# Sixty-four bytes of padding between two SBUF pools of a one-core encoder kernel

## The chip, the cores and the metric

The kernel runs on one core of one Trainium2 chip. The metric is device time in microseconds (us); lower is better. A time is the median of several runs; the rows below come from one profiled execution of the same program.

## What is computed

Two encoder blocks over 256 tokens of 1,024 channels, all in float32. `rms` is a root-mean-square norm with a learned gain. Each mixer has three attention groups (latent attention with 8 heads, windowed attention with 4, neighbourhood attention with 4).

```python
for l in range(2):
    x = x + 0.5 * swiglu(rms(x, ffn1_norm[l]), ffn1_w_in[l], ffn1_w_out[l])      # 1024 -> 2 x 2816 -> 1024
    z = rms(x, mix_norm[l]) @ w_mix_in[l]
    o = concat(rms(latent(z)), rms(windowed(z)), rms(neighbourhood(z)))
    x = x + o @ w_mix_out[l]
    x = x + attention_to_memory(rms(x, mem_norm_x[l]), rms(mem, mem_norm_m[l]))
    x = x + 0.5 * swiglu(rms(x, ffn2_norm[l]), ffn2_w_in[l], ffn2_w_out[l])
    x = rms(x, block_norm[l])
```

## The kernel before

**The weight stream.** All weights come from HBM in pieces of [128 partitions x up to 1,024 floats], in the order of use. `emit_split` (L125) loads a piece into a tile `raw` (pool `rawp`), ScalarE rounds it to float32r as `whi` (L136), and VectorE makes the remainder `wlo` (L137); both lie in the pool `wp`, 7 tiles each. A piece is loaded three ahead of its use. The activations are split in the same way into a high and a low tile, so a product of float32 precision is three float32r matmuls: high by high, high by low, low by high.

**The two ways in which a matmul gets its operands.** TensorE loads one operand as stationary weights (LDWEIGHTS, 128 columns) and streams the other past it. In `mm3` calls of the feed-forward and of the projections (L163 to L165, and L318 for the first columns) the 128x128 block of `whi` or `wlo` is stationary and an activation tile of 256 columns is streamed. In `formb` (L524 to L526), in the two latent up-projections (L699 to L701, L753 to L755) and in the products of the memory tokens it is the other way round: a 128-column block of an activation tile is stationary and 256, 384, 416 or 512 columns of a weight tile are streamed. By the shapes in the code both layers together have 2,384 blocks of the first kind (or memory products) with three matmuls each, 384 matmuls in `formb` and 72 in the up-projections: 7,608 matmuls that pair a weight tile with an activation tile. 7,248 of them stream 256 columns.

**Where tiles lie.** The pools are laid out one after another in each partition: `cp` (residual, gains, constants), `rawp`, `wp`, `sp` (ten slots of 8,192 bytes for the activations), `tp` (working tiles of 128 to 2,048 bytes), `mp` (small ones). A slot of `rawp` or `wp` has 4,096 bytes. The sizes of `rawp`, `wp` and `sp` are multiples of 512 bytes, so every `raw`, `whi`, `wlo` and every activation tile of `sp` starts at the same address modulo 512. A stationary block of 128 floats is 512 bytes and a streamed tile of 256 floats is 1,024, so the operands of nearly every one of these matmuls start at one address modulo 512. The exception is the piece `mb0` in `formb`: it holds two K tiles of 416 columns (1,664 bytes), so the stream of an odd K tile starts 128 bytes further modulo 512 than that of an even one.

**Order.** The framework orders the instructions of each engine by a simulated timeline (`schedule_with_timeline_sim=True`). GpSimd (POOL) starts with small memsets (`nhalf`, L107; a column of ones in `memV`, L541), and waits for the first data after them.

Of the kernel before, what the change touches and what calls it, by code (L numbers as in the profile page):

```python
# [17 lines left out]
L = 2  # L18
# [10 lines left out]
# where in the attention's pipeline (after which head) other work is put in  # L29
# [5 lines left out]
# columns of the per-partition parameter block, per layer  # L35
G_F1, G_MIX, G_MX, G_MM, G_F2, G_BLK, G_GRP, G_CQ, G_HEAD = 0, 8, 16, 24, 32, 40, 48, 56, 59
NG = 67
# columns of the per-token (replicated) parameter block, per layer
# [4 lines left out]
def weight_plan():  # L43
    """Names and widths of the pieces of the weight stream, in the order of use."""
    plan = []
    for l in range(L):
        for name, count, width in (
            ("f1i", 2 * NJ, 1024), ("f1o", NJ, 1024), ("mc", 3, 1024), ("mb0", 4, 832), ("uq", 2, 768),
            ("mb1", 4, 1024), ("ukv", 1, 1024), ("mb2", 4, 768), ("kvk", 2, 1024), ("mo", 8, 1024),
            ("wq", 2, 1024), ("kvv", 2, 1024), ("wo", 2, 1024), ("f2i", 2 * NJ, 1024), ("f2o", NJ, 1024),  # L50
        ):
            plan += [(name, l, i, width) for i in range(count)]
    return plan


def mo_order():
    """(column tile, K tile) of the mixers' output projection: the later groups' K tiles come first."""
    o = [(i, k) for i in range(6) for k in range(4, 8)]
    o += [(i, k) for i in range(6) for k in range(4)]
    return o + [(i, k) for i in range(6, 8) for k in (4, 5, 6, 7, 0, 1, 2, 3)]  # L60
# [8 lines left out]
def encoder_kernel(ctx: ExitStack, tc: tile.TileContext, gxT, memT, wst, bparams, consts, nab, out):  # L69
# [4 lines left out]
    wp = ctx.enter_context(tc.tile_pool(name="wp", bufs=7))  # L74
    sp = ctx.enter_context(tc.tile_pool(name="sp", bufs=10))
    tp = ctx.enter_context(tc.tile_pool(name="tp", bufs=2))
    mp = ctx.enter_context(tc.tile_pool(name="mp", bufs=9))
    pacc = ctx.enter_context(tc.tile_pool(name="pacc", bufs=8, space=PSUM))

# [30 lines left out]
    # the tensor engine's clock is gated until it has been busy for a while: busy it until the first data are there  # L110
# [43 lines left out]
    def units(kind, count):  # L154
        """Successive [128 x 128] blocks of the stream as (hi, lo)."""
        for u in range(count):
            if u % 8 == 0:
                hi, lo = piece(kind)
            o = (u % 8) * P
            yield hi[:, o : o + P], lo[:, o : o + P]  # L160
# [17 lines left out]
    class Normed:  # L178
        """hi / lo parts of (x * gain), tile by tile, and the rows' reciprocal norms.

        With pre, x stands for its own normed value with the gains pre: the rows then have two factors.
        """
# [13 lines left out]
        def _sum(self, v, keep):  # L196
            """Adds up squares, all but the last keep of them."""
            while len(v) > keep + 1:
                if len(v[0]) == 1:
                    t = tp.tile([P, T], F32, tag="sqs", bufs=3, name=self.name + "s")  # L200
                    v[0:2] = [(t, self.eng.tensor_tensor(t, v[0][0], v[1][0], ALU.add))]
                else:
                    t = v[0][0]
                    v[0:2] = [(t, self.eng.tensor_tensor(t, t, v[1][0], ALU.add))]
# [34 lines left out]
        def stats(self, r=None):  # L239
            """Means over the channels (and eps), and the factors from them: [tokens of a half, half]."""  # L240
            self.total()
            ps = acc(self.name + "ps")
            for n, v in enumerate(self.sums):
                for t in range(2):
                    s = slice(t * P, (t + 1) * P)
                    for m, q in enumerate(v):
                        nc.tensor.matmul(
                            ps[:, 2 * n + t : 2 * n + t + 1], q[0][:, s], cmean[:, 0:1],
                            start=m == 0, stop=m == len(v) - 1,
                        )  # L250
            self.m = mp.tile([P, 2], F32, tag="r", name=self.name + "m")
            nc.vector.tensor_scalar(self.m, ps[:, 0:2], EPS, None, ALU.add)
            if self.factor:
                self.r = mp.tile([P, 2], F32, tag="r", name=self.name + "r") if r is None else r
            if self.pre is None:
                if self.factor:
                    rsqrt(self.r, self.m, 2)
                return
            # both norms at once: (m2 / m + eps) ** -0.5 * m ** -0.5 = (m2 + eps * m) ** -0.5
            m2 = small(2, self.name + "m2")  # L260
            nc.vector.scalar_tensor_tensor(m2, self.m, EPS, ps[:, 2:4], ALU.mult, ALU.add)
            self.r0 = mp.tile([P, 2], F32, tag="r", name=self.name + "r0")
            rsqrt(self.r, m2, 2)
            rsqrt(self.r0, self.m, 2)

        def bcast(self):
            """The factors along the tokens, on every partition."""
            rs = [self.r] if self.pre is None else [self.r, self.r0]
            ps = acc(self.name + "pb")
            out = []  # L270
            for n, r in enumerate(rs):
                for t in range(2):
                    o = n * T + t * P
                    nc.tensor.transpose(ps[:, o : o + P], r[:, t : t + 1].to_broadcast([P, P]), ident)
                rb = tp.tile([P, T], F32, tag="rb", name=f"{self.name}rb{n}")
                nc.scalar.copy(rb, ps[:, n * T : (n + 1) * T])
                out.append(rb)
            return out
# [4 lines left out]
    def bc(ap, n):  # L283
        """[P, a, ...] -> [P, a, ..., n] by repetition."""
        return ap.unsqueeze(len(ap.shape)).to_broadcast(list(ap.shape) + [n])

# [1 line left out]
    def ffn(l, which, nx, nxt, hook=None):  # L288
# [18 lines left out]
        for j in range(NJ):  # L307
            if j == 0:
                # the tiles of x may still be in the making: two columns at once, K tile by K tile
# [49 lines left out]
    def project(nm, kind, order, nk, ah, al, nn, hooks={}, late=False):  # L359
        """x += W a in the given order of (column tile, K tile)."""  # L360
# [30 lines left out]
    class Pair:  # L391
        """Two heads whose outputs share a bank; o[:, t, cols[c], :] gets them."""
# [84 lines left out]
    def attend(heads, hooks={}, d1=AT["d1"], d2=AT["d2"]):  # L477
        """Heads in a software pipeline."""
# [16 lines left out]
    def head_factors(nm, hs, n, dim, e):  # L495
        """The heads' factors: of values that are r times what hs [P, 2, n] sums the squares of,
        r * (r ** 2 * hs / dim + eps) ** -0.5 = (hs / dim + e) ** -0.5 with e = eps / r ** 2."""
# [14 lines left out]
    def formb(nm, kind, width, kper, xh, xl, hooks={}):  # L512
        """[tokens, width] products of the next pieces, a bank for each half of the tokens."""
# [16 lines left out]
    def head_squares(nm, ps, a, n, dim, dst):  # L530
        """Sums of squares of n heads from column a of ps into dst."""
# [12 lines left out]
    class Memory:  # L544
        """Keys and values of the memory tokens; their rows' factors serve all layers."""
# [13 lines left out]
        def steps(self, kind, n, done):  # L559
            """The next n of the 16 products (a half of the tokens, a K tile) that make keys or values."""  # L560
# [53 lines left out]
    def mixer(l, nx, mem):  # L614
        nm = f"mx{l}"
        # low-rank projections, transposed
# [17 lines left out]
        # rotary tables with the gains; the softmax scale goes on the queries' gains  # L634
# [18 lines left out]
        # rows' factors of the two latents  # L653
# [18 lines left out]
        # the rotary keys, over the factors of the latent ones  # L672
# [13 lines left out]
        # latent up-projection of the queries  # L686
# [38 lines left out]
        # heads, transposed: two to a block in the windowed and the neighbourhood group  # L725
# [19 lines left out]
        # latent up-projection of the keys and values  # L745
# [29 lines left out]
        # values of the other two groups  # L775
# [25 lines left out]
        for pr in range(2):  # L801
            # heads pr and pr + 2 lie in one block and read the two kv heads
# [80 lines left out]
    def mem_attn(l, nx, mem, nxt):  # L883
# [15 lines left out]
        # the memory tokens' values fill the time until the queries are normed  # L899
# [69 lines left out]
    # the halves of the tokens in banks of their own: only the last tile's squares are waited for  # L969
# [22 lines left out]
def _tiles(v):  # L992
    """[n] -> [128, n / 128]"""
    return v.reshape(-1, P).T


def _pack_weights(inp):
    def units_a(w, order_cols):
        """w [K, N] as [128, 128] blocks, one column tile after another, K inside."""
        K = w.shape[0]  # L1000
        b = w.reshape(K // P, P, w.shape[1] // P, P)
        return b[:, :, order_cols, :].transpose(1, 2, 0, 3).reshape(P, -1)

    def rows(w):
        """w [K, N] -> [128, K / 128 * N]"""
# [5 lines left out]
    def units_in(w):  # L1011
        """Gates and values in turn; the blocks of the first four column tiles go by K tile."""
# [37 lines left out]
def _constants():  # L1050
    """Identity, rotary tables and the windowed group's biases: shapes alone decide them."""
# [17 lines left out]
def _na_bias(rel):  # L1069
    """rel [L, 4, 15, 31] gathered over (query, key); outside the window a constant."""  # L1070
# [56 lines left out]
```

## Time and profile before

| | |
|---|---|
| median of 3 runs | 1081.56 us (1080.64 to 1082.23) |
| profiled execution, first to last instruction | 1081.2 us |
| TensorE busy | 1062.2 us, 98% |
| VectorE, ScalarE, GpSimd busy | 66%, 51%, 11% |
| matmuls in the trace | 8,480 |
| read from HBM | 179.38 MB, 167 GB/s over the span |

The profiled execution shows no time beside its span. Matmuls are pipelined and their ends are modelled, so the times between the starts of matmuls say more than the busy share. PEclk is the granted clock of TensorE in tenths of its upper level (2.4 GHz; the lower one is 1.2 GHz).

### The profile page before, as it was taken

What the parts mean: (1) busy time and instruction counts of PE and PEld (TensorE: products, weight loads), DVE (VectorE), ACT (ScalarE), POOL (GpSimd) and SP (SyncE); (2) the same over time, 40 slices, a digit from 0 to 9 for tenths busy, and PEclk for the clock granted to TensorE, in tenths of its full rate; (3) what the DMA queues carried; (4) which work ended last, traced back from release to release, by engine and by line L of the source; (5) the groups of instructions that cost most, each with busy time, mean ns of one, the idle gap of its engine ahead of it and who ended that gap; (6) DMA issues with size and microseconds to landing.
All of it is one profiled execution on the core that took longest, in us unless ns stands there. A gap on an engine that the chain in (4) does not pass through costs nothing.

```text
span 1081.2 us, 20915 instructions
## 1 busy us (share of the span) xinstructions
PE 1062.2 (98%) x8480; PEld 1041.3 (96%) x8480; DVE 718.1 (66%) x1249; ACT 556.2 (51%) x928; POOL 114.3 (11%) x106
## 2 busy tenths in 40 slices
PE   8999999999999999999999999999999999999996
PEld 7999999998998999999999999999889999999996
DVE  7866667678776676666658665666886776666652
ACT  5644455556563554445445444546674555444441
POOL 4000000062030400000000000001500322000000
PEclk9999999999999999999999999999999999999999
DMA  8855556555032655555555555555531526655641
GB/s 274 274 183 188 176 198 195 170 177 192 21 120 76 231 178 187 184 179 188 181 176 178 191 177 185 202 177 173 175 127 41 156 74 223 189 179 183 187 119 40
DMA packets 54529, 181.79 MB, mean 168 GB/s; under 512 B 6048, under 2 KB 8992, under 8 KB 54432
## 3 DMA queue, kind: packets, MB, share of 16 engines
q1 hardware_dynamic: 54432, 180.45, 52.3%
q8 instruction: 66, 1.08, 0.4%
q14 instruction: 31, 0.25, 0.1%
HBM read 179.38 MB, written 1.05 MB: 167 GB/s over the span
## 4 chain that ended last, share of the span: by engine, by line
PE 73%; issue 17%; DVE 4%; POOL 2%; DMA 2%; ACT 1%; SPq 0%; POOLq 0%; DVEq 0%; ACTq 0%
PE f01i L163 4%; PE f11i L163 4%; PE f01i L165 4%; PE f01i L164 4%; PE f11i L164 4%; PE f11i L165 4%; PE f02i L163 3%; PE f02i L164 3%; PE f02i L165 3%; PE f11o L165 2%; PE f11o L164 2%; PE f11o L163 2%; PE f02o L165 2%; PE f02o L164 2%; PE f02o L163 2%
## 5 line engine op out<-in xcount | busy, mean ns | idle before, releaser
L137 DVE TENSOR_TENSOR wlo<-raw,whi 128x1024 fp32r<-128x1024 f32 (+4 forms) x337 | 407.0, 1211 | 230.7 <-ACT whi L136 229.4
L136 ACT CAST whi<-raw 128x1024 fp32r<-128x1024 f32 (+4 forms) x337 | 343.5, 1022 | 384.4 <-issue 103.9
L163 PE MATMUL f11i<-n10h,whi 128*128 128x256 f32 x320 | 90.8, 284 | 0.0
L163 PE MATMUL f12i<-n21h,whi 128*128 128x256 f32 x320 | 90.7, 284 | 0.0
L163 PE MATMUL f02i<-n20h,whi 128*128 128x256 f32 x320 | 90.7, 283 | 0.0
L163 PE MATMUL f01i<-n0h,whi 128*128 128x256 f32 x320 | 90.7, 283 | 0.0
L165 PE MATMUL f01i<-n0h,wlo 128*128 128x256 f32 x320 | 90.6, 283 | 0.0
L164 PE MATMUL f02i<-n20l,whi 128*128 128x256 f32 x320 | 90.6, 283 | 0.0
L164 PE MATMUL f01i<-n0l,whi 128*128 128x256 f32 x320 | 90.5, 283 | 0.0
L164 PE MATMUL f12i<-n21l,whi 128*128 128x256 f32 x320 | 90.5, 283 | 0.0
L165 PE MATMUL f12i<-n21h,wlo 128*128 128x256 f32 x320 | 90.5, 283 | 0.0
L165 PE MATMUL f02i<-n20h,wlo 128*128 128x256 f32 x320 | 90.5, 283 | 0.0
L164 PE MATMUL f11i<-n10l,whi 128*128 128x256 f32 x320 | 90.5, 283 | 0.0
L165 PE MATMUL f11i<-n10h,wlo 128*128 128x256 f32 x320 | 90.5, 283 | 0.0
L164 PEld LDWEIGHTS f12i<-n21l,whi 128*128 128x128 f32 x320 | 61.4, 192 | 0.0
L164 PEld LDWEIGHTS f02i<-n20l,whi 128*128 128x128 f32 x320 | 61.4, 192 | 0.0
L164 PEld LDWEIGHTS f01i<-n0l,whi 128*128 128x128 f32 x320 | 61.4, 192 | 0.0
L165 PEld LDWEIGHTS f02i<-n20h,wlo 128*128 128x128 f32 x320 | 61.4, 192 | 0.0
L163 PEld LDWEIGHTS f02i<-n20h,whi 128*128 128x128 f32 x320 | 61.4, 192 | 0.0
L164 PEld LDWEIGHTS f11i<-n10l,whi 128*128 128x128 f32 x320 | 61.4, 192 | 0.0
L165 PEld LDWEIGHTS f01i<-n0h,wlo 128*128 128x128 f32 x320 | 61.4, 192 | 0.0
L163 PEld LDWEIGHTS f12i<-n21h,whi 128*128 128x128 f32 x320 | 61.4, 192 | 0.0
(1025 smaller groups left out, 2977.0 us busy)
## 6 DMA issues: line engine op xcount, KB each, us to landing
raw<-in_w SPq DMA_DIRECT2D x311, 512.0 KB, 4.3
raw<-in_w SPq DMA_DIRECT2D x12, 384.0 KB, 3.5
raw<-in_w SPq DMA_DIRECT2D x8, 416.0 KB, 3.2
kv0mt<-in_mem SPq DMA_DIRECT2D x8, 128.0 KB, 4.2
kv1mt<-in_mem SPq DMA_DIRECT2D x8, 128.0 KB, 3.3
gx<-in_gx SPq DMA_DIRECT2D x3, 256.0 KB, 7.2
out<-gx SPq DMA_DIRECT2D x3, 256.0 KB, 2.8
gx<-in_gx SPq DMA_DIRECT2D x1, 323.0 KB, 3.0
```

What stands on the lines that cost most here:

```text
L136: ins = nc.scalar.copy(hi[:, a:b], r[:, a:b])
L137: nc.vector.tensor_tensor(lo[:, a:b], r[:, a:b], hi[:, a:b].bitcast(F32), ALU.subtract)
L163: nc.tensor.matmul(ps, ah, bh, start=first, stop=False)
L164: nc.tensor.matmul(ps, ah, bl, start=False, stop=False)
L165: return nc.tensor.matmul(ps, al, bh, start=False, stop=last)
```

## The change

A pool `pad` with one tile of [128 x 16] float32, 64 bytes in each partition, is put between the weights' pool `wp` and the activations' pool `sp`, and GpSimd fills it with zeros at the start. Nothing reads it. All tiles of `sp`, `tp` and `mp` then lie 64 bytes further in their partitions; `cp`, `rawp` and `wp` stay where they were. The rest of the diff blanks comments and docstrings, line for line, and changes no instruction.

```diff
     wp = ctx.enter_context(tc.tile_pool(name="wp", bufs=7))
+
+    pad = ctx.enter_context(tc.tile_pool(name="pad", bufs=1))
     sp = ctx.enter_context(tc.tile_pool(name="sp", bufs=10))
     tp = ctx.enter_context(tc.tile_pool(name="tp", bufs=2))
     mp = ctx.enter_context(tc.tile_pool(name="mp", bufs=9))
     pacc = ctx.enter_context(tc.tile_pool(name="pacc", bufs=8, space=PSUM))
 
+    nc.gpsimd.memset(pad.tile([P, 16], F32, name="pad"), 0.0)
+
     def slot(shape, dt, name):
```

## Rows read from the trace of the kernel before

**Rows 1.** Page: span, engines (busy us, share, instructions), granted clock in 40 slices.

```profile
span 1081.2 us, 20915 instructions
PE 1062.2 (98%) x8480; PEld 1041.3 (96%) x8480; DVE 718.1 (66%) x1249; ACT 556.2 (51%) x928; POOL 114.3 (11%) x106
...
PEclk9999999999999999999999999999999999999999
```

**Rows 2.** Page: shares of the chain of work that ended last, by engine.

```profile
PE 73%; issue 17%; DVE 4%; POOL 2%; DMA 2%; ACT 1%; SPq 0%; POOLq 0%; DVEq 0%; ACTq 0%
```

**Rows 3.** Stretches: length, busy us (count) of five engines, PEclk, DMA share, GB/s.

```profile
19.00:144.00 125.00, 125.00 (x1044) 125.00 (x1044) 83.54 (x117) 64.31 (x93) 3.57 (x5) 1.00 0.63 207
...
290.00:345.00 55.00, 53.51 (x439) 51.57 (x439) 37.07 (x76) 24.42 (x49) 10.83 (x10) 1.00 0.31 97
345.00:475.00 130.00, 128.90 (x1075) 128.70 (x1074) 86.15 (x129) 67.59 (x102) 12.59 (x8) 1.00 0.56 183
...
540.00:677.00 137.00, 137.00 (x1145) 137.00 (x1145) 86.19 (x128) 64.87 (x96) 2.29 (x2) 1.00 0.56 181
...
1010.00:1074.00 64.00, 61.89 (x517) 61.69 (x515) 27.73 (x40) 23.04 (x32) 0.69 (x1) 1.00 0.35 100
```

**Rows 4.** Timeline of TensorE, feed-forward: first and last of 27 matmuls, 256 columns.

```profile
399.77 0.28 PE L164 MATMUL f02i<-n20l,whi 128*128 128x256 f32 x1
...
400.01 0.28 PE L163 MATMUL f02i<-n20h,whi 128*128 128x256 f32 x1
...
402.89 0.28 PE L163 MATMUL f02i<-n20h,whi 128*128 128x256 f32 x1
```

**Rows 5.** Timeline of the weight loads in the same stretch.

```profile
400.02 0.19 PEld L164 LDWEIGHTS f02i<-n20l,whi 128*128 128x128 f32 x1
```

**Rows 6.** Timeline of TensorE: first and last of 13 matmuls, 384 columns.

```profile
221.73 0.33 PE L701 MATMUL mx0uq<-whi,mx0chl 128*128 128x384 f32 x1
...
223.81 0.33 PE L701 MATMUL mx0uq<-whi,mx0chl 128*128 128x384 f32 x1
```

**Rows 7.** Timeline of TensorE: first and last of 13 matmuls, 512 columns.

```profile
229.24 0.39 PE L526 MATMUL mx0mb<-whi,nx0l 128*128 128x512 f32 x1
...
231.96 0.39 PE L526 MATMUL mx0mb<-whi,nx0l 128*128 128x512 f32 x1
```

**Rows 8.** Timeline of TensorE: each first of six matmuls, 416 columns, K tiles 2 to 7.

```profile
212.15 0.35 PE L524 MATMUL mx0mb<-whi,nx0h 128*128 128x416 f32 x1
...
213.28 0.35 PE L524 MATMUL mx0mb<-whi,nx0h 128*128 128x416 f32 x1
...
214.41 0.35 PE L524 MATMUL mx0mb<-whi,nx0h 128*128 128x416 f32 x1
...
215.54 0.35 PE L524 MATMUL mx0mb<-whi,nx0h 128*128 128x416 f32 x1
...
216.67 0.35 PE L524 MATMUL mx0mb<-whi,nx0h 128*128 128x416 f32 x1
...
217.80 0.35 PE L524 MATMUL mx0mb<-whi,nx0h 128*128 128x416 f32 x1
...
218.93 0.28 PE L658 MATMUL mx0pm<-cmean,mx0csq 128*128 128x1 f32 x2
```

**Rows 9.** Line 214 on VectorE: count, ns min/median/max, first and last start.

```profile
L214 DVE SCALAR_TENSOR_TENSOR nx0l<-gx,nx0h x8: 476/479/484, 148.4 to 203.4; 128x256 fp32r<-128x256 f32 x8
L214 DVE SCALAR_TENSOR_TENSOR kv0l<-kv0mt,gx,kv0h x8: 477/479/486, 151.3 to 206.9; 128x256 fp32r<-128x256 f32 x8
```

**Rows 10.** Line 443: what VectorE waited for longest there (us, times).

```profile
  DMA mx1sw11bt<-in_consts: 1.7, 1
```

**Rows 11.** Timeline of POOL at the start: last memsets, first work (idle before, releaser).

```profile
0.72 0.11 POOL L107 MEMSET nhalf<- 128x16 f32 x1 [0.29 <-POOLq L1117]
0.76 0.11 POOL L541 MEMSET memV<- 128x8 f32 x1
3.84 1.28 POOL L644 TENSOR_SCALAR mx0gq<-gx 128x1 f32<-128x1 f32 x3 [2.97 <-DMA gx<-in_gx]
```

## The prediction

> **What bounds the kernel now.** I read the page first. TensorE is busy for 98% of the span at the upper clock level, 2.4 GHz, in all forty slices, and VectorE, ScalarE and POOL for 66%, 51% and 11% [rows 1]. The chain of work that ended last is TensorE's for 73% and "issue" for 17%, time in which the engine waits for nothing that the profile shows [rows 2]; in a full TensorE stream, that is the piece of each step which the modelled matmul does not explain. The table by stretches then says where this holds: in the feed-forwards TensorE has no gap at all (1,044 matmuls in 125 us, 1,145 in 137 us, 119.7 ns each). Gaps appear around the attention and at the starts and ends of norms, and are small: 1.5, 1.1 and 2.1 us in the stretches shown [rows 3].
>
> So the time is a count of matmuls times the step from one start to the next, and the timeline gives that step. With 256 columns, 26 steps take 3.12 us: 120.0 ns [rows 4]. The 7,248 matmuls of this width alone make 7,248 x 0.120 = 870 us of the 1081.2. With 384 columns, 12 steps take 2.08 us, 173.3 ns [rows 6]; with 512 columns, 2.72 us, 226.7 ns [rows 7]. The differences are 53.3 ns for each 128 columns, which at 2.4 GHz is one column a cycle. Taking that off (106.7, 160.0 and 213.3 ns) leaves the same 13.3 ns in all three: a fixed part of each matmul, 11% of a step of 120 ns. The next weights are loaded while a matmul streams (a load starts at 400.02 us, the matmul before it at 400.01) [rows 4, 5]. Nothing but a change of the 120 ns can move this kernel much.
>
> **The change, part by part.**
>
> *The shift between stationary and streamed operands.* It touches each of the 7,608 matmuls that pair a weight tile with an activation tile: before, both start at one address modulo 512; after, they are 64 bytes apart. It does not touch pairs of two activation tiles (scores, values), which move together, nor the split of the weights, whose three tiles stay. The price is 7,608 times the change of the step. Each 0.1 ns is 0.76 us, so 0.28 ns would be 0.2% of the time (2.2 us), about what a measurement of this kernel can tell from no change, since the three runs shown span 1.6 us.
>
> No row shows a matmul with a 64-byte shift. The nearest are those of 416 columns, where odd K tiles stream from 128 bytes further than even ones, against the same stationary phase. Six matmuls of an even K tile take 1.13 us and six of an odd one 1.13 us, in all six groups from 212.15 to 218.93 us: 188.3 ns each [rows 8]. Rounded to 0.01 us in six, the two kinds differ by at most 1.7 ns each. And the fixed part of 13.3 ns is one number for 256, 384 and 512 columns, though the streams end at different times against the load that runs beside them [rows 4, 6, 7]. A collision of two reads in one stretch of 512 bytes should show in one of these; a fixed cost of changing the weights would look just like this.
>
> Bounds, then: 1.7 ns on either side by that row, 7,608 x 1.7 = 12.9 us, so 1068 to 1094 us. The row is also what I take the value from: its two phases agree to the last digit shown, so 0 ns and 0 us. 416 columns also has the odd cost that 188.3 - 173.3 = 15.0 ns remain there instead of 13.3. It is the only width that is no multiple of 128 columns, and I come back to it as a rival.
>
> *The other engines' operands.* VectorE and ScalarE read and write the shifted tiles beside unshifted ones (`x`, the gains). The remainder of line 214 reads `x` from `cp` in one group and a memory tile from `tp` in another, 264 bytes apart modulo 512 by the sizes in the code: 479 ns both, 476 to 486 in all [rows 9]. I take 0. If each shifted operation cost 2% more, VectorE would still be idle for a third of the time [rows 1]; where it ends a wait, those 2% of 0.48 us are 0.01 us for each link of the chain. VectorE's 4% of it, 43 us, would give 0.9 us [rows 2].
>
> *DMAs.* The stream into `raw` keeps its addresses, as do the residual and the output. Sixteen loads of memory tiles and sixteen of biases land 64 bytes further. Before, the longest wait at line 443 for a bias was 1.7 us, once [rows 10]. I cost the change at 0, hidden by loading three heads ahead; uncovered it would be a part of such a wait, below 1 us.
>
> *The memset.* One more instruction on POOL, of `nhalf`'s shape: 0.11 us, with 0.04 us from start to start there. It stands before two memsets that nobody waits for soon, and POOL then sits for 2.97 us until the first data land at 3.84 us [rows 11]. Cost 0; without that cover 0.11 us. It queues no DMA and adds no wait to another engine, and `sp` keeps its slots.
>
> Sum: 1081.2 + 0 + 0 + 0 + 0 = 1081.2 us for a profiled execution. The median of the runs is 0.4 us above that, so 1081.6 us.
>
> **The rivals.**
>
> *The fixed part is a collision, and the shift ends it (faster).* In every pair of operands of the three clean widths, both start at one phase, and the next weights are read while the stream runs [rows 4, 5]. If the 13.3 ns were the two reads meeting in the same part of 512 bytes, 64 bytes could free them: up to 7,608 x 13.3 = 101 us, 980 us. For it: no row has another phase than 0 or 128 bytes. Against it: at 128 bytes the step did not fall [rows 8]. It decides as soon as a step falls by 0.28 ns. The Trainium skill, TensorE: Matmul & The Clock Gate, section Back-to-back issue gap, gives an isolated matmul 1/2.4 ns a column plus 2.5 ns, 109.2 ns for 256 columns. By that rule all but 2.5 ns of the fixed part is avoidable, and an estimate by it would be 1081.6 - 7,608 x 10.8 ns = 999 us; the trace's 120.0 ns does not agree with it for this stream.
>
> *A stream out of step with the loads costs more (slower).* With 416 columns, where a stream's end does not fall on a multiple of 512 bytes, the remainder is 15.0 ns instead of 13.3 [rows 4, 8]. If that is the price of a stream and a load that do not start at one phase, the shift puts it on all 7,608: 1.7 x 7,608 = 12.9 us, 1094.5 us, decided from 0.28 ns on. For it: that row; against it: there the end is out of step and not the start, and the odd K tiles, whose start is, cost the same as the even.
>
> *A small gain by the same lever.* The mirror of it, up to 12.9 us, 1068.7 us.
>
> *Another order.* The framework plans with a simulated timeline, and a memset at its start, if it shifted one wait there, could swap instructions. The price would be one exposed gap like those of 1.1 to 2.1 us [rows 3]: 1082.7 to 1083.7 us.
>
> *The change doesn't shift.* If the allocator rounds the pool up to 512 bytes, nothing moves: 1081.6 us.
>
> The Trainium skill, SBUF — State Buffer, section Who interferes with whom, gives TensorE two SBUF read ports of its own, one for the stream and one for the weights, and has it wait for nobody. By that rule the first three rivals fall away and the time stays at 1081.6 us. The equal steps of even and odd K tiles agree [rows 8], but no row here has 64 bytes.
>
> **How the numbers follow.** No change of the step, or no shift: 0.67, 1081.6 us, with 1079.4 to 1083.8 as its own range. The slower rival 0.12, the collision that ends 0.12, the small gain 0.05, another order 0.04, three quarters of it within 0.2%. That gives faster by over 0.2% 0.12 + 0.05 = 0.17, within 0.2% 0.67 + 0.03 = 0.70, slower 0.12 + 0.01 = 0.13. The range reaches to the bounds of the unknown step, 1068 to 1095 us, and leaves out the collision that ends, of 0.12.
>
> **What would show it.** The timeline of a feed-forward with 120.0 ns from start to start, six matmuls of 416 columns in 1.13 us, 479 ns at line 214, and 13.3 ns left at 384 and 512 columns would show each step right. A step of 121.7 ns or of 118.3 everywhere speaks for the two small rivals, one near 107 to 109 for the collision. Unequal steps in one feed-forward and not in another would mean that the phase matters together with something I haven't read. Equal steps with another sum would mean another order. My prediction is wrong if 64 bytes, which no row tried, are not like 128.

## The result and the profile after

The changed kernel takes 1067.39 us (median of four runs, 1066.59 to 1071.27) and the kernel before 1081.1 us beside it (1080.58 to 1082.23): a ratio of 0.988, 95% interval 0.986 to 0.990. It is 13.7 us faster. The profiled execution of the changed kernel took 1071.27 us itself, the slowest of the four, with a span of 1069.5 us. Its lines are numbered four higher than those of before, so L163 is now L167.

The page of the changed kernel: span, engines, granted clock in 40 slices, and the chain of work that ended last.

```profile
span 1069.5 us, 20916 instructions
...
PE 1048.8 (98%) x8480; PEld 1027.0 (96%) x8480; DVE 717.6 (67%) x1249; ACT 556.9 (52%) x928; POOL 114.5 (11%) x107
...
PEclk9999999999999999999999999999999999999998
...
PE 75%; issue 17%; DVE 4%; DMA 2%; ACT 1%; POOL 1%; SPq 0%; POOLq 0%; DVEq 0%; ACTq 0%
```

The same number of matmuls, VectorE and ScalarE instructions run, one POOL instruction more, and the shares hardly moved [rows 1, 2]. TensorE alone has become 13.4 us less busy. The table by stretches shows it at work without a gap in the feed-forwards, as before [rows 3], but with more matmuls in the same time: 121 us hold 1,031 (117.4 ns each), 136 us hold 1,158 (117.4), where it was 119.7. (Columns: length, busy us and count of PE, PEld, DVE, ACT, POOL, granted clock, DMA share, GB/s.)

```profile
19.00:140.00 121.00, 121.00 (x1031) 121.00 (x1030) 82.33 (x116) 63.02 (x93) 2.54 (x3) 1.00 0.67 212
...
363.40:366.80 3.40, 3.40 (x19) 3.40 (x18) 1.04 (x1) 0.00 (x0) 1.61 (x1) 0.53 0.69 225
534.00:670.00 136.00, 136.00 (x1158) 136.00 (x1157) 87.52 (x131) 66.50 (x99) 2.29 (x2) 1.00 0.57 185
889.10:892.50 3.40, 3.40 (x18) 3.40 (x18) 0.62 (x1) 1.04 (x1) 0.00 (x0) 0.53 0.87 299
```

The timeline of TensorE in the changed kernel, the first and the last of each row of equal matmuls (start, us, engine, line, operation, output and operands):

```profile
209.88 0.38 PE L528 MATMUL mx0mb<-whi,nx0h 128*128 128x416 f32 x1
...
211.04 0.35 PE L528 MATMUL mx0mb<-whi,nx0h 128*128 128x416 f32 x1
...
212.18 0.38 PE L528 MATMUL mx0mb<-whi,nx0h 128*128 128x416 f32 x1
...
213.34 0.35 PE L528 MATMUL mx0mb<-whi,nx0h 128*128 128x416 f32 x1
...
214.47 0.28 PE L662 MATMUL mx0pm<-cmean,mx0csq 128*128 128x1 f32 x2
...
215.71 0.34 PE L705 MATMUL mx0uq<-whi,mx0chl 128*128 128x384 f32 x1
...
217.79 0.34 PE L705 MATMUL mx0uq<-whi,mx0chl 128*128 128x384 f32 x1
...
219.52 0.39 PE L528 MATMUL mx0mb<-whi,nx0h 128*128 128x512 f32 x1
...
222.32 0.39 PE L528 MATMUL mx0mb<-whi,nx0h 128*128 128x512 f32 x1
...
362.21 0.61 PE L251 MATMUL n20ps<-cmean,n20s 128*128 128x1 f32 x4 [1.68 <-POOL n20s L208]
...
363.22 0.42 PE L168 MATMUL f02i<-n20l,whi 128*128 128x256 f32 x1
...
366.63 0.28 PE L169 MATMUL f02i<-n20h,wlo 128*128 128x256 f32 x1
...
394.78 0.28 PE L169 MATMUL f02i<-n20h,wlo 128*128 128x256 f32 x1
...
397.84 0.28 PE L168 MATMUL f02i<-n20l,whi 128*128 128x256 f32 x1
```

- **256 columns, activations streamed** (the 6,960 matmuls of the feed-forwards and projections): 26 steps in 3.06 us, 117.7 ns, where it was 120.0 [rows 4]. Over all 2,112 matmuls of the feed-forwards' output projections the mean is 117.78 ns.
- **384 columns, weights streamed**: in the query projection 12 steps in 2.08 us, 173.3 ns, as before [rows 6]. In the other product of this width, in `formb`, the first layer has 12 steps in 2.12 us, 176.7 ns; the second has 173.3 again. Before, both settled at 173.3.

```profile
234.18 0.34 PE L528 MATMUL mx0mb<-whi,nx0h 128*128 128x384 f32 x1
...
236.30 0.34 PE L528 MATMUL mx0mb<-whi,nx0h 128*128 128x384 f32 x1
```

- **512 columns, weights streamed**: 12 steps in 2.80 us, 233.3 ns, and so 6.6 ns slower [rows 7].
- **416 columns**: six matmuls of an even K tile (from 209.88 and 212.18 us) take 1.16 us, six of an odd one (from 211.04 and 213.34) 1.14 and 1.13. Before, both took 1.13 [rows 8].

So the padding changed the step of nearly everything that streams past weights, in both directions. The sum, with those steps: 6,960 x -2.2 ns = -15.3 us; the 96 query projections of the memory attention, 120 to 114 ns, -0.6; 192 products of the memory tokens, -0.4; 120 matmuls of 512 columns, +0.8; those of 416 columns, +0.2; the 48 of 384 columns in the first layer, 3.3 ns each, +0.2: together -15.1 us. Part of it is given back. TensorE waits a little longer for the sums of squares from POOL at the two norms ahead of a second feed-forward (1.7 us, as at 362.21, and 2.1 us; before 1.1 and 1.3), 1.4 us more. And after each of those gaps the granted clock falls to the lower of its two levels, 1.2 GHz, for 3.4 us (0.53 over the stretch): 16 steps from 363.22 to 366.63 take 3.41 us, 213 ns each, 1.53 us more than at 117.8, twice. -15.1 + 1.4 + 3.1 = -10.6 us; the profiled spans differ by 11.7. The other runs, 3.4 to 4.7 us faster than this one, met fewer such stretches, by their mean granted clock of 0.996 to 0.997 against 0.994 here (one stretch at half the clock is 0.0016 of the span). The execution of before that was profiled had none [rows 1].

The length of the gap doesn't settle whether the clock falls. In minus64, a kernel of the next section, the gap at the same place was longer, and the clock stayed at the upper level:

```profile
355.18 0.61 PE L249 MATMUL n20ps<-cmean,n20s 128*128 128x1 f32 x4 [2.01 <-POOL n20s L206]
```

```profile
355.20:358.60 3.40, 3.40 (x29) 1.00 0.88 300
```

At the lower level the fixed part of the step is gone: 213 ns are 256 cycles at 1.2 GHz, one for each column. Whether that holds at distance 0 isn't shown: in the feed-forwards of the kernel before the record has no stretch at the lower level.

What the prediction costed at nothing did stay at nothing. Line 218 on VectorE (count; ns at least, in the median, at most):

```profile
L218 DVE SCALAR_TENSOR_TENSOR nx0l<-gx,nx0h x8: 477/480/484, 145.1 to 199.3; 128x256 fp32r<-128x256 f32 x8
L218 DVE SCALAR_TENSOR_TENSOR kv0l<-kv0mt,gx,kv0h x8: 478/480/486, 147.9 to 203.1; 128x256 fp32r<-128x256 f32 x8
```

The wait for a bias at line 447 (longest, us, and times), and POOL at the start:

```profile
  DMA mx1sw11bt<-in_consts: 1.6, 1
```

```profile
0.72 0.11 POOL L82 MEMSET pad<- 128x16 f32 x1 [0.29 <-POOLq L1121]
0.76 0.11 POOL L111 MEMSET nhalf<- 128x16 f32 x1
...
3.85 1.28 POOL L648 TENSOR_SCALAR mx0gq<-gx 128x1 f32<-128x1 f32 x3 [2.94 <-DMA gx<-in_gx]
```

480 ns for 479 [rows 9], 1.6 us for 1.7 [rows 10], and the memset vanishes in a wait of 2.94 us [rows 11].

### The profile page after: what moved, and what is told of

Its sections match the earlier page's. It is cut to its first block, busy times and chain, and to the rows that moved or that the text cites. A ratio compares the mean times of both kernels' runs of the same rounds, so it can differ in the third digit from the quotient of the medians.

```text
span 1069.5 us, 20916 instructions
## 1 busy us (share of the span) xinstructions
PE 1048.8 (98%) x8480; PEld 1027.0 (96%) x8480; DVE 717.6 (67%) x1249; ACT 556.9 (52%) x928; POOL 114.5 (11%) x107
## 4 chain that ended last, share of the span: by engine, by line
PE 75%; issue 17%; DVE 4%; DMA 2%; ACT 1%; POOL 1%; SPq 0%; POOLq 0%; DVEq 0%; ACTq 0%
PE f11i L167 4%; PE f01i L167 4%; PE f01i L169 4%; PE f11i L169 4%; PE f11i L168 3%; PE f01i L168 3%; PE f02i L167 3%; PE f02i L169 3%; PE f02i L168 3%; PE f11o L167 2%; PE f02o L167 2%; PE f01o L167 2%; PE f11o L169 2%; PE f02o L169 2%; PE f01o L169 2%
## 5 line engine op out<-in xcount | busy, mean ns | idle before, releaser
L167 PE MATMUL f02i<-n20h,whi 128*128 128x256 f32 x320 | 90.5, 283 | 0.0
L167 PE MATMUL f12i<-n21h,whi 128*128 128x256 f32 x320 | 90.2, 282 | 0.0
L167 PE MATMUL f11i<-n10h,whi 128*128 128x256 f32 x320 | 89.9, 281 | 0.0
L167 PE MATMUL f01i<-n0h,whi 128*128 128x256 f32 x320 | 89.8, 281 | 0.0
L167 PEld LDWEIGHTS f12i<-n21h,whi 128*128 128x128 f32 x320 | 60.9, 190 | 0.0
L167 PEld LDWEIGHTS f02i<-n20h,whi 128*128 128x128 f32 x320 | 60.8, 190 | 0.0
L169 PEld LDWEIGHTS f12i<-n21h,wlo 128*128 128x128 f32 x320 | 60.6, 189 | 0.0
L169 PEld LDWEIGHTS f11i<-n10h,wlo 128*128 128x128 f32 x320 | 60.2, 188 | 0.0
```

What stands on the lines that cost most here:

```text
L167: nc.tensor.matmul(ps, ah, bh, start=first, stop=False)
L169: return nc.tensor.matmul(ps, al, bh, start=False, stop=last)
```

## The experiments

**The theory:** the step of these matmuls depends on how far the streamed tile starts from the stationary block, modulo some power of two. The rivals: it depends on where the activations themselves lie; the padding or its memset merely changed the order or the timing of something; or the changed step is an accident of one execution. "Distance" below is the start of the streamed tile less that of the stationary block, modulo 512 bytes, for the products with streamed activations: 0 before, +64 in the changed kernel. Where weights are streamed, the same padding gives the other sign, -64 in the changed kernel. The kernels differ in the lines that lay out the pools; `pad(n)` is a pool with a tile of n floats, set to zero by POOL as in the change. Each time without a range is of one execution. The kernel before took 1081.51 us beside the first eight, 1084.72 beside minus32, mixed, kick6 and kickall, and 1082.64 (median of seven, 1081.06 to 1084.77) beside the last four.

### Where the padding lies

```diff
# all64: everything moves, the distance stays 0
+pad(16)
 rawp, wp, sp, tp, mp
# end64: nothing moves
 rawp, wp, sp, tp, mp
+pad(16)
# plus256: pools in another order, no padding; distance 256
-rawp, wp, sp, tp, mp
+rawp, sp, tp, wp, mp
```

> The same 64 bytes of padding, but ahead of the raw tiles' pool, so that weight tiles and activation tiles move together: absolute addresses are those of the changed kernel for the activations, while stream and stationary block start at one address modulo 512 again. Theory A (the distance between the two operands modulo 512 sets the step): 120.0 ns from start to start in the feed-forwards, 1081 us. Theory B (the absolute address of the streamed tile sets it): 117.8 ns, 1067 us. Theory C (the memset or the order of the instructions did it): 1067 us.

> Padding and memset as in the changed kernel, but behind the last pool, so that no tile moves. Theories A and B: 120.0 ns a step, 1081 us. Theory C (memset, order): 117.8 ns, 1067 us.

> The weights' pool comes behind the activations' and the working tiles' pools, whose sizes put it 256 bytes apart modulo 512, without any padding. Theory D (period of 128 bytes): as at 128 bytes, 118.7 ns, 1074 us. Theory F (period of 512 bytes, the farthest distance): 118.7 ns or more if the gain fades with the distance, or the lowest step if what counts is being far from 0.

all64 took 1081.76 us, end64 1081.68 and plus256 1082.59, all at a mean step of 120.00 ns. The timeline of the second feed-forward, 27 matmuls in all64:

```profile
399.81 0.28 PE L166 MATMUL f02i<-n20l,whi 128*128 128x256 f32 x1
...
402.93 0.28 PE L165 MATMUL f02i<-n20h,whi 128*128 128x256 f32 x1
```

and in plus256:

```profile
399.76 0.28 PE L163 MATMUL f02i<-n20h,whi 128*128 128x256 f32 x1
...
402.88 0.28 PE L165 MATMUL f02i<-n20h,wlo 128*128 128x256 f32 x1
```

26 steps in 3.12 us in both. In all64 the activations lie exactly where the changed kernel has them modulo 512, and the memset is there too: neither the activations' own address nor the memset nor the order is the lever. The distance is, and 256 bytes count as none. It is no accident of one execution either: the slowest of the four runs of the changed kernel (1071.27 us) is 9.3 us below the fastest of the four of before (1080.58).

The same distance also lies between what TensorE streams and the tiles that ScalarE and VectorE write. Their work is not the cause: by the starts in the traces, 137 of the 2,108 steps in the feed-forwards' output projections of before had none of VectorE, ScalarE and POOL at work from 0.3 us ahead of them to their end, and 130 of those in the changed kernel. Their means are 120.0 and 117.8 ns, those of all the others as well.

### The size of the distance

```diff
# plus32, plus96, plus128, plus160: n = 8, 24, 32, 40
 rawp, wp
+pad(n)
 sp, tp, mp
# minus64, minus32: n = 16, 8
-rawp, wp, sp, tp, mp
+rawp, sp, pad(n), wp, tp, mp
```

> 32 bytes between the weights' and the activations' pool. So far the feed-forward step is 120.0 ns at 0 bytes, 113.3 or 117.8 at 64 bytes either way, about 118.7 in no fixed rhythm at 128. Theory D (distance modulo 128 sets it, with 64 the best): 32 bytes lie between 0 and 64, 116 to 119 ns, 1060 to 1075 us. Theory E (only distances of 64 bytes and more count, whatever the period): 120.0 ns, 1081 us.

> 96 bytes between the two pools. Theory D (period of 128 bytes): as with 32 bytes, and as 32 bytes the other way. Theory F (period of 512 bytes, best near 64 and worse from there on): between 64 and 128 bytes, 117.8 to 118.7 ns, 1067 to 1074 us.

> Padding of 128 bytes between the same two pools. Theory A, growing with the distance: twice the gain, 115.5 ns a step, about 1053 us. Theory A with a period of 128 bytes, as the equal steps of even and odd K tiles of 416 columns suggested before: 120.0 ns, 1081 us. A threshold (any distance is enough): 117.8 ns, 1067 us.

> 160 bytes between the two pools. Theory D (period of 128 bytes): as with 32 bytes. Theory F (period of 512 bytes): at or above the 118.7 ns of 128 bytes, 1074 to 1081 us.

> As minus64, with 32 bytes in place of 64: the streamed activation tiles lie 32 bytes less far than the weight tiles. So far, by distance: 0 bytes 120.0 ns, 32 bytes 116.7, 64 bytes 117.8 or 113.3, 96 bytes 120.0, 128 bytes 118.7, 160 bytes 118.0, 256 bytes 120.0 in the same fixed rhythm as 0. Theory G (period of 256 bytes, no mirror image): -32 is 224 bytes, not yet seen; anything between 113 and 120 ns, 1045 to 1081 us. Theory H (period of 256 bytes, and the sign does not matter): 116.7 ns as with 32 bytes, 1062 us.

> The weights' pool comes behind the activations' pool and the 64 bytes lie between them: the streamed activation tiles lie 64 bytes less far modulo 512 than the weight tiles, instead of further. Theory A with a sign (only a stream that is ahead of the weights gains, as the 512-column streams of weights, which became 64 bytes short, went from 226.7 to about 233 ns): the feed-forward step does not fall and may rise to some 126 ns, 1081 to 1125 us. Theory A without a sign (any distance will do): 117.8 ns, 1067 us. Theory B (absolute address of the streamed tile, which is as before): 120.0 ns, 1081 us.

Mean step in the 2,112 matmuls of the feed-forwards' output projections, and the time:

| distance | step, ns | us |
|---|---|---|
| 0 (before, all64) | 120.00 | 1081.51, 1081.76 |
| +32 | 116.67 | 1062.42 |
| +64 (the change) | 117.78 | 1067.39 (median) |
| +96 | 120.00, single steps 116 to 125 | 1083.93 |
| +128 | 118.66 | 1073.81 |
| +160 | 118.66 in two of four feed-forwards, 117.33 in two; mean 118.00 | 1070.85 |
| 256 | 120.00 | 1082.59 |
| -64 | 113.33 in one of four feed-forwards, 117.78 in three | 1060.92 |
| -32 | 118.33 | 1073.26 (before beside it: 1084.72) |

The stretch from 410 to 470 us, all in one feed-forward, shows the same by counting. (Columns: length, PE busy and count, granted clock, DMA share, GB/s.) plus32:

```profile
410.00:470.00 60.00, 60.00 (x517) 1.00 0.55 186
```

plus96:

```profile
410.00:470.00 60.00, 60.00 (x503) 1.00 0.54 181
```

plus128:

```profile
410.00:470.00 60.00, 60.00 (x508) 1.00 0.54 185
```

TensorE is busy throughout at the upper clock level in all three, and DMA moves about the same; 60 us at 120.0 ns would be 500 matmuls. The curve has no order by size: 32 bytes help more than 64, 96 bytes don't help the mean at all, and the sign matters (+64 and -64, +32 and -32 differ). That 96 bytes leave the mean where it was while they spread single steps from 116 to 125 ns says that the fixed rhythm of 120.0 is not what costs. No theory put down beforehand gave this curve: +96, +128 and +160 lie outside all of them, and -32 only inside the one that allowed anything from 113 to 120 ns.

### The two rhythms

minus64 left two step lengths in one execution. Its table by stretches, first and second feed-forward:

```profile
70.00:140.00 70.00, 70.00 (x620) 1.00 0.56 192
410.00:470.00 60.00, 60.00 (x512) 1.00 0.55 187
```

70 us / 620 = 112.9 ns and 60 us / 512 = 117.2; over whole projections 113.33 and 117.78. At 2.4 GHz 113.33 ns are 272 cycles, 16 more than the columns; the 120.0 of before are 288, 32 more. The kernel holds a control for this: in the output projection of the memory attention the streamed tiles lie in `tp`, which minus64 leaves at distance 0 from the weights, as before. Its timeline there, a few microseconds from matmuls at 113.3:

```profile
333.39 1.00 PE L165 MATMUL me0wo<-me0oh,whi 128*128 128x256 f32 x7
...
334.23 0.28 PE L166 MATMUL me0wo<-me0ol,whi 128*128 128x256 f32 x1
```

Seven steps in 0.84 us: still 120.0 ns.

The next kernels ask which pair of operands counts, and what chooses the rhythm.

```diff
# mixed: wlo 64 bytes off against sp, whi at distance 0
-rawp, wp, sp, tp, mp
+rawp, wh, sp, pad(16), wl, tp, mp        # hi from wh, lo from wl
# kick6: minus64, and in each feed-forward, ahead of column tile 6
 ps = acc(f"{nm}i{j}")
+if j == 6: nc.tensor.transpose(ps[:, 0:P], ident, ident)
# kickall: minus64, and ahead of every column tile from 6 on
+if j >= 6: nc.tensor.transpose(ps[:, 0:P], ident, ident)
```

The transpositions write into a bank that the next matmul overwrites; they add work and change no output.

> Two pools for the weight tiles: whi starts at the same address modulo 512 as the activation tiles, wlo 64 bytes further. In the feed-forward the matmuls follow each other as whi by high, whi by low, wlo by high. Theory I (the stream meets the load of the NEXT weights): the step of whi by low, beside which wlo is loaded, falls to 113 to 118 ns, the other two stay at 120.0; 1066 to 1076 us. Theory J (the stream meets its own weights' phase): the step that follows wlo by high falls instead. Theory K (any change of distance breaks the rhythm for all three): all three change.

> minus64 with one more, useless, 128-column transposition of the identity ahead of column tile 6 in each of the four feed-forwards (into a bank that is overwritten). In minus64 the first feed-forward ran at 113.3 ns throughout, the other three at 117.8 from the last interruption on. Theory L (at 64 bytes there are two rhythms, an interruption picks one, and it holds until the next): after the added matmul the three slow feed-forwards have a new chance; if one falls to 113.3 ns it gains some 1,280 x 4.5 ns = 5.8 us, and the first may lose as much; 1043 to 1067 us. Theory M (the step belongs to the stage, its tiles' addresses or the load on the other engines): each stage keeps its step, 1062 us with 4 x 0.3 us for the added matmuls.

> As kick6, but with an added transposition ahead of every column tile from 6 to 21 in each of the four feed-forwards, 64 in all, some 0.3 us each, 19 us together. Theory L: the step changes between 113.3 and 117.8 ns at some of these 64 places and is constant between two of them. Theory M: it does not depend on them.

mixed took 1069.31 us. Its three matmuls of a product have means of 117.5, 117.5 and 118.3 ns, though only the one with `wlo` has a new distance to its own weights, and only one streams while the next `wlo` is loaded. The step is thus no sum over single pairs; the stream of loads and matmuls settles as a whole.

kick6 took 1054.98 us, kickall 1067.4. In kick6 the single dummy operation in the third feed-forward (at 561.4 us) moved it from the one rhythm into the other, and there it stayed: by its table, 137 matmuls in the 16 us before and 311 in 35 us after, 112.5 ns each, where the plain kernel of distance -64 has 299. First two stretches of kick6, then one of minus64:

```profile
544.00:560.00 16.00, 16.00 (x137) 1.00 0.44 161
565.00:600.00 35.00, 35.00 (x311) 1.00 0.61 197
```

```profile
565.00:600.00 35.00, 35.00 (x299) 1.00 0.56 192
```

In the second and the fourth feed-forward it went the other way, from 113.3 to 117.8. kickall shows the change at one operation (its timeline in the first feed-forward):

```profile
59.98 0.28 PE L166 MATMUL f01i<-n0l,whi 128*128 128x256 f32 x1
...
60.69 0.28 PE L166 MATMUL f01i<-n0l,whi 128*128 128x256 f32 x1
...
60.93 0.27 PE L329 MATMUL f01i<-ident 128*128 128x128 f32 x1
...
61.97 0.28 PE L167 MATMUL f01i<-n0h,wlo 128*128 128x256 f32 x1
...
62.99 0.28 PE L167 MATMUL f01i<-n0h,wlo 128*128 128x256 f32 x1
```

Six steps in 0.71 us ahead of it, 118 ns; nine in 1.02 after it, 113.3. There the rhythm changes only at such operations, and in a pattern: of four successive column tiles in the first feed-forward one runs at 113.3 and three at 117.8 (those at 113.3 start at 61, 84, 107 and 130 us). Here an interruption can change the rhythm, and between two of them it holds.

The last four kernels time the two fast ones, try interruptions of another shape, and ask whether the changed kernel has the fast rhythm too.

```diff
# minus64_timed, kick6_timed: the same programs, timed
# kickstat: minus64; ahead of column tile 6 of the last three feed-forwards
+for c in range(4): nc.tensor.matmul(ps[:, c:c+1], ident, cmean[:, 0:1], start=True, stop=True)
# plus64_kick6: the changed kernel with the operation of kick6
+if j == 6: nc.tensor.transpose(ps[:, 0:P], ident, ident)
```

> minus64 again, now timed against the kernel before: the 64 bytes the other way round, 1061 us in one run, ratio 0.981. Theory L (each interruption picks a rhythm by chance of a few nanoseconds): the runs differ among themselves by several us, more than the 1.6 us of the kernel before. Theory M (the step belongs to the stage): they agree within 2 us.

> kick6 again, timed: 1055 us in one run beside 1084.7 for the kernel before, ratio 0.973. Theory L: it stays faster than the kernel before by 2 to 3%, with a spread of several us between runs, since the added transposition of the second and the fourth feed-forward can fall either way. Theory M: 1062 us, as minus64.

> minus64 with another interruption ahead of column tile 6 of the feed-forwards 2, 3 and 4: four one-column float32 matmuls of the kind that the norm's statistics make, as those after column tile 2 of the first feed-forward, which ended in the rhythm of 113.3 ns in each of four traces. Theory L': this kind of interruption leads to 113.3 ns: all three feed-forwards take it, 1040 to 1045 us. Theory L (any interruption picks by chance): one or two of them do, 1045 to 1062 us.

> The changed kernel's padding with the four added transpositions of kick6. In its trace one stretch of the last feed-forward ran at 113.3 ns and everything else at 117.8. Theory L with either sign of the 64 bytes: one or more of the four feed-forwards fall to 113.3 ns after the added transposition, 1045 to 1066 us. Theory N (at +64 bytes the slow rhythm is the lasting one): 117.8 ns throughout, 1068 us.

minus64_timed took 1050.99 us (median of four, 1047.28 to 1054.55; ratio 0.971, interval 0.968 to 0.975), kick6_timed 1052.06 (1049.52 to 1060.73; 0.973, 0.968 to 0.977). The operation of kick6 brings nothing that can be told from its absence. In the profile of minus64_timed the second feed-forward now ran in the fast rhythm, with no edit between it and minus64:

```profile
410.00:470.00 60.00, 60.00 (x531) 1.00 0.58 195
```

531 against 512. Three feed-forwards of four ran at 113.3 in that execution (1047.92 us) and one of four in minus64 (1060.92). By 1,584 matmuls x 4.45 ns, one feed-forward's rhythm is worth 7.0 us, two 14.1; the two executions differ by 13.0. So the spread of this kernel's times, 7.3 us over four runs, has the size of one feed-forward's rhythm; the rhythms themselves were seen in the two profiled executions and not in the other three. kickstat took 1064.56 us: all three feed-forwards ran at 113.3 ahead of its four small matmuls and at 117.8 after them. Nine microseconds of the second feed-forward on either side:

```profile
364.00:373.00 9.00, 9.00 (x82) 1.00 0.51 177
376.00:385.00 9.00, 9.00 (x78) 1.00 0.51 179
```

So the theory that such an interruption, like the norms' small matmuls, leads back into the fast rhythm falls, and so does the other one put down, by which one or two of the three would be fast. plus64_kick6 took 1068.54 us, at 117.8 ns before and after the operation:

```profile
410.00:470.00 60.00, 60.00 (x512) 1.00 0.55 187
```

At +64 the rhythm of 117.8 lasts nearly everywhere; in the feed-forwards of the changed kernel 113.3 is seen from 871 to 889 us alone, some 140 matmuls. At -64 both can last. That stretch also shows that it takes no interruption to change the rhythm. It began in the midst of the last feed-forward's first matmuls, with no other operation of TensorE between them:

```profile
868.23 1.10 PE L322 MATMUL f12s<-n21h,whi 128*128 128x256 f32 x8
...
870.11 1.09 PE L322 MATMUL f12s<-n21l,whi 128*128 128x256 f32 x8
871.04 1.07 PE L322 MATMUL f12s<-n21h,whi 128*128 128x256 f32 x8
871.95 1.07 PE L322 MATMUL f12s<-n21h,wlo 128*128 128x256 f32 x8
```

Sixteen steps in 1.88 us (117.5 ns), then eight in 0.91 (113.8).

## Why the prediction was wrong

**What held.** The frame did: the time is a count of matmuls times their step, and only that step could move the kernel much. The price held too: 0.1 ns for 0.76 us on 7,608 matmuls, and the time followed the measured steps (-15.1 us by the sum, -13.7 by the medians, with 4.5 us given back in the profiled execution, to longer waits and a lower clock, terms that the prediction's sum did not have). VectorE, the DMAs, the memset and the order were rightly put at nothing. The doubt in the last sentence, that 64 bytes are not like 128, was justified, and one of the signs came: unequal steps within one kernel, "that the phase matters together with something I haven't read".

**The step that failed** is "The row is also what I take the value from: its two phases agree to the last digit shown, so 0 ns and 0 us", and the bound of 1.7 ns with it. The row of 416 columns stood for another case: it streams weights past an activation, in another width. Nor is it as even as it looked. Each six was read from two starts rounded to 0.01 us, so two sixes can differ by 0.02 us, 3.3 ns each and not 1.7; and by the starts in nanoseconds the six of an even K tile take 1,130 and 1,124 ns, those of an odd one 1,136. Between 1,124 and 1,136 lie 2.0 ns a matmul, and single steps go from 183 to 194, where those of the feed-forwards' output projections are 120 throughout. A difference of distance was in the row, below the rounding. Asked of the 256-column matmuls themselves, 128 bytes gave 118.66 ns instead of 120.00 (plus128), and 64 bytes 117.78, a fall of 2.2 ns where the bound had 1.7. In the changed kernel the row of 416 columns itself splits, into 1.16 and 1.13 to 1.14 us, and 512 columns pay 6.6 ns, while 384 pay 3.4 in one product and nothing in the other three: one width says little of another.

**The second argument** failed too: that a collision "should show in one of these", since the fixed part is 13.3 ns at 256, 384 and 512 columns alike. All three were read at distance 0. A cost that is the same in all widths at one distance can still be a cost of the distance.

**The rivals.** The collision that ends, with a chance of 0.12 and 980 us, was right in direction and wrong in size, and whether two reads collide is not shown: 64 bytes freed 2.2 of the 13.3 ns, and the best rhythm seen anywhere, at -64, frees 6.7 and leaves 6.7. The small gain, chance 0.05 and 1068.7 us, is what came, but its size agrees by luck: its 1.7 ns was what 416 columns cost above 384, taken with the other sign, and has nothing to do with the 2.2 ns measured at 256 columns. The slower stream has no case at 64 bytes in the 256-column matmuls, and has one in those of 512 columns. Padding that shifts nothing is what end64 shows, not the change.

**Two rules against the runs.** The Trainium skill, SBUF — State Buffer, section Who interferes with whom, has the stream and the weights read through independent ports and TensorE wait for nobody; by that the change would alter nothing. The runs do not agree for these float32r streams: with nothing but the distance changed, the step goes from 120.0 to 113.3. The Trainium skill, TensorE: Matmul & The Clock Gate, section Back-to-back issue gap, gives an isolated matmul 1/2.4 ns a column plus 2.5 ns, an estimate of 109.2 ns for 256 columns; the stream comes nearer to it and does not reach it, with 113.3 at best.

**What stays open.** That the step depends on the distance is shown, and also that the distance alone does not fix it (two steps at -64 and at +160). That two reads meet in the memory is one reading of it and not shown. Nothing here shows whether 256 bytes are a period (0 and 256 are the only two that agree), why 96 bytes give the old mean with uneven steps, or what chooses one rhythm or the other. Distances that are no multiple of 32 bytes, and those from 192 to 224, 288 to 416, were not tried.

## What to carry to other kernels

Where a kernel is a dense stream of matmuls, the relative start of streamed and stationary tiles is a parameter like a tile size: sweep it in both signs, by padding between pools, since here it was worth 1.2% in the change and 2.9% at its best (1050.99 us with `sp`, 64 bytes and then `wp`), and no size predicted its neighbour. Where two rhythms are possible, take several runs: one run of the distance -64 gave 1060.92 us, another 1047.28. A fixed part of a step that is equal in several shapes is no proof of a fixed cost, as long as all of them share the layout. And a bound taken from a row holds for that row's width and roles alone; where everything hangs on one number, widen it by what the nearest row differs in.

## What the runs showed of the hardware

- The step of 256-column float32r matmuls with changing weights is 120.00 ns when both operands start at one address modulo 256, and 113.3 to 118.7 in mean at +32, +64, +128, +160, -64 and -32 bytes; at +96 it is 120.00 in mean and 116 to 125 singly (TensorE at the upper clock level throughout the stretches counted).
- The sign counts: 116.67 at +32 and 118.33 at -32; +64 keeps 117.78 but for some 140 matmuls of one execution, -64 has both 113.33 and 117.78.
- The rhythm of such a stream can persist: in minus64_timed, 113.3 ns held over the whole stretch shown, 531 matmuls, and one 128-column operation put another such stream into or out of it. Two executions of one program (minus64 and minus64_timed) differ by 13.0 us, with the fast rhythm in one and in three of four feed-forwards, 7.0 us each.
- The changed distance, -64 for streamed weights, made 512-column matmuls with streamed weights slower, 226.7 to 233.3 ns, and left 384 columns at 173.3 in three of four products, with 176.7 in one.
- After gaps of 1.7 and 2.1 us the granted clock of the changed kernel fell to the lower level for 3.4 us, 213 ns a step; in the execution of before, with gaps of 1.1 and 1.3 us there, it did not, nor in that of minus64, with 2.0 and 2.1. In those stretches a step has no fixed part: 213 ns for 256 columns at 1.2 GHz.
